# Three products of high and low parts for the softmax attentions, and an earlier start of the third block of w_out

## The chip, the cores and the metric

The kernel runs on one core of one Trainium2 chip. The metric is the device time of one execution in microseconds, as the median of several runs. The profile is one more execution of the same program, recorded by the hardware profiler.

## What is computed

Two layers of a hybrid decoder trunk over 256 positions of width 2048, all in float32. In each layer one projection of the normalised input feeds four groups of four heads: forgetting attention (fox), differential attention (diff), block-sparse attention (moba) and gated linear attention (GLA). Each group's output is multiplied by a SiLU gate, the four are joined and mapped back by w_out. Cut to what the change touches:

```python
def forgetting_attention(q, k, v, log_f):      # head width 128, 128-query blocks
    logits = einsum("bhqd,bhkd->bhqk", q_i, k) * scale + c_i[..., :, None] - cum[:, :, None, :]
    logits = where(k_pos <= q_pos, logits, -inf)
    return einsum("bhqk,bhkd->bhqd", softmax(logits), v)

p = softmax(q1 k1^T) - lam * softmax(q2 k2^T)  # differential attention, causal
diff = einsum("bhqk,bhkd->bhqd", p, v)

# block-sparse attention: with 256 positions there is one block of 256 keys,
# so each query attends to its own block, causally
moba = einsum("bhql,bhld->bhqd", softmax(where(own_pos <= q_pos, q k^T * scale, -inf)), v)

mixed = concatenate([fox, diff, moba, gla], axis=-1)
x = x + einsum("bse,ed->bsd", mixed, w_out)
```

## The kernel before

**Two kinds of product.** A large product (projection by w_in, output by w_out) is made of three F32R products of high and low parts: a weight tile `raw` that arrives by DMA is rounded into `hi` by ScalarE (`hi_of`, L399), the rest goes into `lo` by VectorE (`lo_of`, L402), and the input side stands ready as two tiles as well (`hTp` for the normalised input, `mTh` and `mTl` for the mixed output). `multiply` (L1194) issues hi by high, hi by low and lo by high. The small products of the attentions (scores and P V) take plain F32 operands, one `matmul` each (L275).

**The weight stream.** `_blocks` (L95) lists for each layer 17 column blocks of w_in and four of w_out (the last of the second layer is cut in two). A block sums 16 k tiles of 128 rows, in steps of two k tiles for a block of 512 columns, 12 products a step, and of four for narrower blocks. `_steps` (L131) orders the steps. Blocks with a `turn` go together: a turn's cut points say after which k tiles of a block the others have their turn. For w_out the turn is `(12,)` for the blocks 0 and 1, and the k tiles come in the order of the groups 3, 0, 1, 2 (GLA, fox, diff, moba). So the first 12 k tiles of block 0 go first, then the first 12 of block 1, then the last four of block 0 and of block 1, which are moba's, then the blocks 2 and 3. A block accumulates in one of two PSUM tiles `mm`, or, for one block of w_in whose `"side"` is set (L1082), in one of the two `side` tiles that the attentions use.

**Tasks between steps.** The rest of a layer runs as Python generators in `tasks`. After each step `tick` (L258) lets each task go on to its next `yield`, as long as the instructions that they have issued on VectorE and ScalarE cost no more, by a model, than the PE time issued so far. `prepare` (L1249) issues the split of the step three ahead, and at most four steps have parts. If a step needs k tiles that no task has finished yet, the loop at L1287 lets the tasks run on without PE steps between.

**Steps of a softmax group.** `projected` (L489) takes a projection out of PSUM, rotates it where needed, and turns it by 32x32 transposes and a transfer through DRAM (`turned`, `moved`, L284 and L297). For the queries `natural_of` (L481) makes one more copy into the plain order. `softmax` (L721) issues 12 score products a layer, `normalised` (L780) and `turned_p` (L763) divide and turn P, and `attend_columns` (L793) issues the 12 P V products of fox and moba, after it has waited for the values and the gate. `diff` (L890) issues its own, with 64-row score products that the change leaves alone, and 12 P V products. The values come out of PSUM in `fox_first`, `fox_v` and `rows_v` (L821, L832, L881), one ScalarE copy for each half of the rows. A group's output goes into its four k tiles of `mTh` and `mTl` in `split_group` (L524).

**Buffers.** `s4` has nine slots of 1024 elements a partition (`T4`), `s2` seven of 512 (`T2`). P turned is the fixed tile `pT`, which `env["pT"]` hands from one group to the next. GLA's masked queries are the fixed tile `tq` (L329), cleared once at the start on GpSimd (L1150); before that its space holds part of the first inputs.

Of the kernel before, what the change touches and what calls it, by code (L numbers as in the profile page):

```python
# [13 lines left out]
F32 = mybir.dt.float32  # L14
# [23 lines left out]
X_AT = (24, 28, 32, 36)  # L38
T4 = 9
T2 = 7  # L40
LAND = 5
# [53 lines left out]
def _blocks():  # L95

    def block(w, l, c0, n, kind, groups=(0, 1, 2, 3), turn=None):
        kts = [g * 4 + i for g in groups for i in range(4)]
        return {"w": w, "l": l, "c0": c0, "n": n, "kind": kind, "kts": kts, "per": 4 if n * 4 <= STEP_W else 2, "turn": turn}

    out = []
    for l in range(DEPTH):
        for i, (c0, n) in enumerate((
            (COL["gla_a"], 264),
            (COL["gla_g"] + 248, 264),
            (COL["gla_q"], 512),
            (COL["gla_v"], 512),
            (COL["fox_v"] + 258, 258),
            (COL["fox_q"], 512),
            (COL["fox_k"], 512),  # L110
            (COL["diff_q"], 512),
            (COL["diff_k"], 512),
            (COL["fox_v"], 258),
            (COL["fox_g"], 512),
            (COL["diff_v"], 512),
            (COL["moba_q"], 512),
            (COL["moba_k"], 512),
            (COL["diff_g"], 512),
            (COL["moba_g"], 512),
            (COL["moba_v"], 512),  # L120
        )):
            out.append(block("w_in", l, c0, n, "rows", turn=(l, (4, 8, 12)) if i < 3 else None))
        for chunk in range(4):
            cut = l + 1 == DEPTH and chunk == 3
            out.append(block("w_out", l, chunk * 512, 256 if cut else 512, "rows", (3, 0, 1, 2),
                             turn=(DEPTH + l, (12,)) if chunk < 2 else None))
    out.append(block("w_out", DEPTH - 1, D - 256, 256, "apart", (3, 0, 1, 2)))
    return out
# [35 lines left out]
class Costed:  # L164
# [5 lines left out]
    def __getattr__(self, name):  # L170
        f = getattr(self.eng, name)

        def call(*args, **kw):
            n = max(int(np.prod(a.shape[1:])) for a in args if hasattr(a, "shape"))
            self.us += self.fixed + self.per * n
            return f(*args, **kw)  # L176

        return call


# [25 lines left out]
def hybrid_trunk(  # L206
# [33 lines left out]
    s8 = Slots(wk, "eight", 1)  # L240
    sgs = Slots(wk, "gate", 2)
    side = Slots(sd, "side", 2)

# [31 lines left out]
    def matmul(out, lhsT, rhs, start, stop, tiles=1):  # L275
        left["pe"] += int(np.prod(rhs.shape[1:])) * (4 if lhsT.dtype == F32 else 1) / 2400.0 / tiles
        t_.matmul(out, lhsT, rhs, start=start, stop=stop)  # L277

    def transpose(out, src):
# [48 lines left out]
    ls2 = cp.tile([P, DEPTH, 2], F32, name="ls2")  # L328
    tq_flat = cp.tile([P, 2 * NL * P], F32, name="tq")  # L329
    tq = tq_flat.rearrange("p (m l x c) -> p m l x c", m=2, l=NL, x=2)  # L330
    one = cp.tile([P, 1], F32, name="one")
# [100 lines left out]
    def make_hT(l, chunk, parts):  # L432
# [23 lines left out]
        squares(l, chunk, parts)  # L456
        yield from moved(t, 2, X_LAND)
        tk = t.rearrange("p q j (k m) -> p k m (q j)", m=2)
# [29 lines left out]

    def projected(name, pool=None, heads_first=False, func=AF.Copy, turn=None, natural=None):  # L489

        def done(l, ps):
            nat = s4.get([P, 8, P])
            rows_of(l, ps, nat.rearrange("p (a m) d -> p m a d" if heads_first else "p (m a) d -> p m a d", m=2), func)
            tasks.append(run(l, nat))
            return nat

        def run(l, nat):
            yield
            if turn is not None:
                yield from rotated(nat, *turn)  # L500
            t = yield from turned([nat], pool or s4, lambda: s4.put(nat))
            if natural:
                t = yield from natural_of(t, s4, natural)
                yield
            env[name, l] = t
            ready.add((name, l))

        return done

    def rotated(nat, name, half, width):  # L510
# [99 lines left out]
    def gla(l, an):  # L610
        yield from until("constants")
        yield
        ps = yield from take_side()
# [31 lines left out]
        for pair in range(2):  # L645
# [56 lines left out]
            side.put(px)  # L702
        s4.put(env["gla_qk", l])
        s2.put(cum)
        yield from until(("gla_v", l))
# [15 lines left out]
    def softmax(qT, kT, scale, su, forget):  # L721
# [3 lines left out]
        for m in range(2):  # L725
            for kt in range(m + 1):
                dst = S[m][:, kt]
                for h in range(H):
                    matmul(dst[:, h], qT[:, m * H + h], kT[:, :, kt * H + h], True, True)
        s4.put(qT, kT)  # L730
        yield
# [48 lines left out]
    def normalised(p0, p1, su):  # L780
# [10 lines left out]
        return t  # L791

    def attend_columns(l, gi, name, qT, kT, forget=None):  # L793

# [4 lines left out]
        yield from until((name + "_v", l))  # L799
        yield from until((name + "_g", l))  # L800
        yield
        vn, sgT = env[name + "_v", l], env[name + "_g", l]
        ops = yield from take_side()
        o = ops.rearrange("p (h t) -> p h t", h=H)
        for h in range(H):
            v0, v1 = vn[:, 0, h * P:(h + 1) * P], vn[:, 1, h * P:(h + 1) * P]
            matmul(o[:, h, :P], v0, t[:, h], True, True)
            matmul(o[:, h, P:], v0, t[:, H + 2 * h], True, False)
            matmul(o[:, h, P:], v1, t[:, H + 2 * h + 1], False, True)
        s4.put(vn)  # L810
        env["pT"] = t
        yield
        mixed = yield from s4.take([P, H, SEQ])
        by_q = [z.rearrange("p h (m q j) -> p q (h m) j", m=2, q=4) for z in (mixed, o)]
# [4 lines left out]
        yield from split_group(l, gi, mixed, lambda: s4.put(mixed))  # L819

    def fox_first(l, ps):  # L821
        r = env["r", l]
        vn = s4.get([P, 2, GW])
        fx = sm.tile([P, 2, H], F32, name="fx", bufs=2)
        for m in range(2):
            v_.tensor_scalar(fx[:, m], ps[m][:, 254:258], r[:, m:m + 1], None, op0=OP.mult)
            a_.activation(vn[:, m, 258:], ps[m][:, :254], AF.Copy, scale=r[:, m:m + 1])
        env["fox_v", l] = vn
        tasks.append(fox(l))
        tasks.append(fox_forget(l, fx))  # L830

    def fox_v(l, ps):  # L832
        r, vn = env["r", l], env["fox_v", l]
        for m in range(2):
            a_.activation(vn[:, m, :258], ps[m], AF.Copy, scale=r[:, m:m + 1])
        ready.add(("fox_v", l))
# [44 lines left out]
    def rows_v(name):  # L881
        def done(l, ps):
            vn = s4.get([P, 2, GW])
            rows_of(l, ps, vn)
            env[name, l] = vn
            ready.add((name, l))

        return done

    def diff(l):  # L890
# [6 lines left out]

        def product(dst, i, h, m, kt):
            rows = slice(i * 64, i * 64 + 64)
# [12 lines left out]
        for h in range(H):  # L912
            for i in range(2):
                product(S[:, i, h], i, h, 0, 0)
        yield
# [17 lines left out]
        for kt in range(2):  # L933
            for h in range(H):
                for i in range(2):
                    product(T[i][:, kt, h], i, h, 1, kt)
        s4.put(qT, kT)
# [31 lines left out]
        yield  # L969
        vn = env["diff_v", l]  # L970
        ops = yield from take_side()
        o = ops.rearrange("p (m h d) -> p m h d", m=2, h=H)
        for h in range(H):
            matmul(o[:, 0, h], z[:, h], vn[:, 0, h * P:(h + 1) * P], True, True)
        for h in range(H):
            matmul(o[:, 1, h], z[:, H + 2 * h], vn[:, 0, h * P:(h + 1) * P], True, False)
            matmul(o[:, 1, h], z[:, H + 2 * h + 1], vn[:, 1, h * P:(h + 1) * P], False, True)
        s4.put(vn)
        env["pT"] = z
        yield  # L980
# [75 lines left out]
    for l in range(DEPTH):  # L1056
# [3 lines left out]
            gla_first, gla_gate, gla_qk, gla_v, fox_first,  # L1060
            projected("fox_q", natural=whole),
            projected("fox_k"),
            projected("diff_q", turn=turn_d, natural=whole),
# [3 lines left out]
            rows_v("diff_v"),  # L1067
            projected("moba_q", turn=turn_m, natural=whole),
            started(moba, projected("moba_k", turn=turn_m)),
            diff_gate,  # L1070
# [7 lines left out]
    for z in _BLOCKS:  # L1078
        l, f = next(dones)
        blocks.append({"kind": z["kind"], "lhs": hT if z["w"] == "w_in" else mT, "n": z["n"], "per": z["per"], "done": f and partial(f, l),  # L1080
                       "keys": {("r", l)}, "need": "h" if z["w"] == "w_in" else "m", "l": l,
                       "side": z["turn"] is not None and z["c0"] == COL["gla_g"] + 248})  # L1082
    plan = []
# [6 lines left out]
    def bundle(half):  # L1090
        return (pT, tq_flat)[half][:, :first.shape[2]]

# [45 lines left out]
    def first_rms():  # L1138
# [5 lines left out]
        for c in range(4):  # L1144
            yield from until(("h", 0, c))
            if c == 0:
                for half in range(2):
                    a_.activation(xts[0][:, half * 2:half * 2 + 2].rearrange("p k t -> p (k t)"),
                                  bundle(half)[:, KT:KT + 2 * SEQ], AF.Square)
                g_.memset(tq, 0.0)  # L1150
                g_.memset(pT, 0.0)
# [178 lines left out]
```

## Time and profile before

| | us |
|---|---|
| median of 3 runs | 910.52 (910.34 to 910.62) |
| the profiled execution | 910.29 |
| its span, first to last instruction | 908.5 |
| PE busy | 898.7 |
| VectorE (DVE) busy | 632.6 |
| ScalarE (ACT) busy | 497.9 |
| GpSimd (POOL) busy | 91.1 |

PE is the matmul engine, PEld its weight loads, which overlap with its products. A record of the trace is one instruction; matmuls are pipelined, so that a record is longer than its share of the engine's time. The chain of the page follows the work that ended last back to its start, and gives each engine its share of it.

### The profile page before, as it was taken

How to read it: one execution, taken by the hardware profiler on the slowest of the kernel's cores; microseconds unless marked ns; L12 is line 12 of the kernel's file. 1: busy time of each engine (PE TensorE's matmuls, PEld its weight loads, DVE VectorE, ACT ScalarE, POOL GpSimd, SP SyncE). 2: the span in 40 equal slices, each digit the busy share in tenths (PEclk: the TensorE clock that was granted, in tenths of full speed). 3: DMA queues.
4: the chain of work that ended last, by engine and by line, in shares of the span. 5: the costliest groups of instructions: out<-in, count | busy, mean ns of one | idle time of the engine just before them, and what ended most of it. 6: DMA issues, size and time to landing. Idle time of an engine off the chain costs nothing.

```text
span 908.5 us, 12645 instructions
## 1 busy us (share of the span) xinstructions
PE 898.7 (99%) x4678; PEld 766.0 (84%) x4678; DVE 632.6 (70%) x972; ACT 497.9 (55%) x679; POOL 91.1 (10%) x149
## 2 busy tenths in 40 slices
PE   9999999999999999999999999999999999999996
PEld 7989888898888888888899898888888888888886
DVE  7756778688568667746764658886875785695662
ACT  7576754465455357445665674644645545654441
POOL 1010011120101111001200101012200001220000
PEclk9999999999999999999999999999999999999999
DMA  9776576677747757758965756676866576686552
GB/s 325 246 235 195 183 267 223 214 234 210 250 141 232 231 187 228 231 170 260 295 198 178 239 172 238 184 229 214 254 218 199 162 234 200 216 270 213 187 165 93
DMA packets 56508, 195.78 MB, mean 215 GB/s; under 512 B 7637, under 2 KB 7933, under 8 KB 56446
## 3 DMA queue, kind: packets, MB, share of 16 engines
q1 hardware_dynamic: 45760, 164.47, 55.9%
q0 software_dynamic: 9616, 29.38, 11.3%
q10 hardware_dynamic: 1070, 1.14, 0.4%
q8 instruction: 36, 0.59, 0.3%
q14 instruction: 26, 0.21, 0.1%
HBM read 179.74 MB, written 15.21 MB: 215 GB/s over the span
## 4 chain that ended last, share of the span: by engine, by line
PE 98%; issue 1%; DMA 1%; DVE 0%; ACT 0%; POOLq 0%; POOL 0%; DVEq 0%; SPq 0%; ACTq 0%
PE mm L277 89%; PE side L277 9%; DMA tq<-in_first 1%; PE side L281 0%; DVE xs L176 0%; DVE hTp L176 0%; ACT hi L176 0%; DVE lo L176 0%; POOLq L1326 0%; POOL rf L397 0%; ACT two L176 0%; ACT hTp L176 0%; DVEq L1326 0%; SPq L1111 0%; DVE ssf L176 0%
## 5 line engine op out<-in xcount | busy, mean ns | idle before, releaser
L176 DVE TENSOR_TENSOR lo<-raw,hi 128x1024 fp32r<-128x1024 f32 (+2 forms) x299 | 364.8, 1224 | 236.2 <-ACT hi L176 234.1
L176 ACT ACTIVATE hi<-raw 128x1024 fp32r<-128x1024 f32 (+2 forms) x299 | 316.8, 1062 | 367.3 <-PE mm L277 318.4
L277 PE MATMUL mm<-hi,hTp 128*128 128x512 f32 (+2 forms) x2048 | 465.5, 371 | 0.1
L277 PEld LDWEIGHTS mm<-hi,hTp 128*128 128x128 f32 x2048 | 358.3, 188 | 65.9 <-issue 0.7
L277 PE MATMUL mm<-lo,hTp 128*128 128x512 f32 (+2 forms) x1024 | 249.8, 369 | 0.2
L277 PEld LDWEIGHTS mm<-lo,hTp 128*128 128x128 f32 x1024 | 181.0, 188 | 33.2 <-DVE lo L176 0.6
L277 PE MATMUL mm<-hi,mTh 128*128 128x512 f32 (+1 forms) x256 | 95.2, 376 | 0.0
L277 PE MATMUL mm<-hi,mTl 128*128 128x512 f32 (+1 forms) x256 | 95.0, 376 | 0.0
L277 PE MATMUL mm<-lo,mTh 128*128 128x512 f32 (+1 forms) x256 | 64.4, 376 | 0.0
L305 POOL DMA_DIRECT2D four<-turn x84 | 46.0, 554 | 102.3 <-DMA turn<-four 51.7
L277 PEld LDWEIGHTS mm<-hi,mTh 128*128 128x128 f32 x256 | 48.2, 188 | 8.7
L277 PEld LDWEIGHTS mm<-hi,mTl 128*128 128x128 f32 x256 | 48.2, 188 | 8.7
L277 PEld LDWEIGHTS mm<-lo,mTh 128*128 128x128 f32 x256 | 46.2, 188 | 8.7
L301 POOL DMA_DIRECT2D turn<-four x21 | 12.1, 577 | 320.0 <-DVE four L176 319.9
L176 DVE STREAM_TRANSPOSE pT<-four 32x128 f32<-32x128 f32 (+1 forms) x116 | 39.3, 350 | 1.0
L176 ACT ACTIVATE four<-mm,rstd 128x512 f32<-128x512 f32 (+2 forms) x56 | 33.5, 646 | 3.6 <-DVE fx L176 3.5
L176 ACT ACT_TABLE_LOAD x24 | 30.8, 1283 | 3.3 <-DVE an L176 3.0
L277 PEld LDWEIGHTS side<-four,four 128*128 128x128 f32 (+1 forms) x224 | 21.4, 190 | 1.9 <-issue 1.4
L277 PE MATMUL side<-four,four 128*128 128x128 f32 (+1 forms) x224 | 22.7, 277 | 0.0
L176 DVE STREAM_TRANSPOSE four<-four 128x1024 f32<-128x1024 f32 x18 | 22.3, 1240 | 0.3
L176 ACT ACTIVATE four<-side,nb 128x256 f32<-128x256 f32 (+1 forms) x48 | 20.6, 446 | 1.3 <-DVE nb L176 1.2
L176 DVE COPY_PREDICATED four<-masks,side 128x128 f32<-128x128 uint8 x56 | 19.1, 342 | 2.1 <-PE side L277 0.3
(149 smaller groups left out, 536.9 us busy)
## 6 DMA issues: line engine op xcount, KB each, us to landing
raw<-in_weights SPq DMA_DIRECT2D x272, 512.0 KB, 4.2
turn<-four POOLq DMA_DIRECT2D x21, 512.0 KB, 4.7
four<-turn POOLq DMA_DIRECT2D x84, 128.0 KB, 4.5
raw<-in_weights SPq DMA_DIRECT2D x16, 516.0 KB, 4.4
raw<-in_weights SPq DMA_DIRECT2D x15, 528.0 KB, 4.9
turn<-gate POOLq DMA_DIRECT2D x4, 512.0 KB, 5.5
gate<-turn POOLq DMA_DIRECT2D x16, 128.0 KB, 5.6
four<-in_xt SPq DMA_DIRECT2D x3, 512.0 KB, 6.5
```

The lines of the kernel that those rows point to most:

```text
L176: return f(*args, **kw)
L277: t_.matmul(out, lhsT, rhs, start=start, stop=stop)
L301: g_.dma_start(via, t.rearrange("p c a b -> p c (a b)"))
L305: g_.dma_start(t[c * 32:(c + 1) * 32].rearrange("p q a b -> p q (a b)"), via[:, c].rearrange("(q i) e -> i q e", q=4))
```

## The change

The scores of fox and moba and the P V of fox, diff and moba become sums of three F32R products:

```diff
+    def pairs(a, b):
+        return [(a[0], b[0]), (a[0], b[1]), (a[1], b[0])]
+
+    def product(out, a, b, start=True, stop=True):
+        both = pairs(a, b)
+        for i, (x, y) in enumerate(both):
+            matmul(out, x, y, start and i == 0, stop and i == len(both) - 1)
...
-                    matmul(dst[:, h], qT[:, m * H + h], kT[:, :, kt * H + h], True, True)
+                    product(dst[:, h], qT(m * H + h), kT(kt * H + h))
...
-            matmul(o[:, h, :P], v0, t[:, h], True, True)
-            matmul(o[:, h, P:], v0, t[:, H + 2 * h], True, False)
-            matmul(o[:, h, P:], v1, t[:, H + 2 * h + 1], False, True)
+            product(o[:, h, :P], v0, t(h))
+            product(o[:, h, P:], v0, t(H + 2 * h), stop=False)
+            product(o[:, h, P:], v1, t(H + 2 * h + 1), start=False)
...
-            matmul(o[:, 0, h], z[:, h], vn[:, 0, h * P:(h + 1) * P], True, True)
+            product(o[:, 0, h], z(h), vn((0, h)))
```

An `Operand` holds the two tiles and gives the two parts of one piece. The queries and keys of fox and moba are split after they are turned (for the queries this takes the place of `natural_of`), P after it is turned, the values as they leave PSUM:

```diff
+    def in_parts(t, side_of):
+        if side_of == "k":
+            hi = yield from s4.take(t.shape, F32R)
+            hi_of(hi, t)
+            yield
+            lo = yield from s4.take(t.shape, F32R)
+            lo_of(lo, t, hi)
+            s4.put(t)
+            return Operand((hi, lo), lambda n: (hi[:, :, n], lo[:, :, n]))
+        hi = yield from s4.take([P, t.shape[2], P], F32R)
+        lo = yield from s4.take([P, t.shape[2], P], F32R)
+        by_q = [z.rearrange("p n (q j) -> p q n j", q=4) for z in (hi, lo)]
+        for q in range(4):
+            hi_of(by_q[0][:, q], t[:, q])
+        yield
+        for q in range(4):
+            lo_of(by_q[1][:, q], t[:, q], by_q[0][:, q])
+        s4.put(t)
+        return Operand((hi, lo), lambda n: (hi[:, n], lo[:, n]))
...
+    def p_operand(t, vn):
+        h0 = yield from s2.take([P, H, P], F32R)
+        h1 = yield from s4.take([P, 2 * H, P], F32R)
+        hi_of(h0, t[:, :H])
+        hi_of(h1, t[:, H:])
+        yield
+        lo = yield from tqs.take([P, 3 * H, P], F32R)
+        lo_of(lo[:, :H], t[:, :H], h0)
+        lo_of(lo[:, H:], t[:, H:], h1)
+        env["pT"] = t
+        yield
+        return Operand((h0, h1, lo), lambda n: (h0[:, n] if n < H else h1[:, n - H], lo[:, n]))
...
+    def parts_of_v(l, ps, vn, c, to):
+        r = env["r", l]
+        for m in range(2):
+            a_.activation(vn[0][:, m, to], ps[m][:, c], AF.Copy, scale=r[:, m:m + 1])
+        for m in range(2):
+            v_.scalar_tensor_tensor(vn[1][:, m, to], ps[m][:, c], r[:, m:m + 1], vn[0][:, m, to].bitcast(F32), op0=OP.mult, op1=OP.subtract)
```

In `attend_columns` the wait for the gate stays ahead of P V for fox alone, and stands behind it for moba. `tq` becomes a slot of its own (`tqs`) that GLA takes and clears in each layer and gives back after its products, and that then holds the low part of P. The counts of the slots change, and a chunk's wait:

```diff
-T4 = 9
-T2 = 7
+T4 = 10
+T2 = 5
...
+    tqs = Slots(wk, "tq", 1)
...
-        yield from moved(t, 2, X_LAND)
+        yield from moved(t, 2, X_LAND if chunk else LAND)
...
+        tq_flat = yield from tqs.take([P, 2 * NL * P])
+        g_.memset(tq_flat, 0.0)
...
-                g_.memset(tq, 0.0)
+                tqs.put(first_tq)
```

Of w_out's third block the first four k tiles (GLA's) are put ahead of moba's k tiles of the blocks 0 and 1, and its sum is held in a `side` tile:

```diff
-                             turn=(DEPTH + l, (12,)) if chunk < 2 else None))
+                             turn=(DEPTH + l, ((12, 12), (12, 12), (0, 4, 4))[chunk]) if chunk < 3 else None))
...
-                       "side": z["turn"] is not None and z["c0"] == COL["gla_g"] + 248})
+                       "side": (z["w"], z["c0"]) in (("w_in", COL["gla_g"] + 248), ("w_out", 1024))})
```

More of the change, by code (lines that the diff above doesn't have):

```diff
@@ L178, in __getattr__, with __init__, __call__ @@
         return call
+class Operand:
+    def __init__(self, tiles, get):
+        self.tiles, self.get = tiles, get
+    def __call__(self, n):
+        return self.get(n)
 class Slots:
@@ L328, in hybrid_trunk @@
     ls2 = cp.tile([P, DEPTH, 2], F32, name="ls2")
-    tq_flat = cp.tile([P, 2 * NL * P], F32, name="tq")
-    tq = tq_flat.rearrange("p (m l x c) -> p m l x c", m=2, l=NL, x=2)
+    first_tq = tqs.get([P, 2 * NL * P])
     one = cp.tile([P, 1], F32, name="one")
@@ L487, in natural_of, with projected @@
         return z
-    def projected(name, pool=None, heads_first=False, func=AF.Copy, turn=None, natural=None):
+    def projected(name, pool=None, heads_first=False, func=AF.Copy, turn=None, natural=None, side_of=None):
         def done(l, ps):
@@ L504, in run @@
                 yield
+            elif side_of:
+                t = yield from in_parts(t, side_of)
+                yield
             env[name, l] = t
@@ L611, in gla @@
         yield from until("constants")
+        tq_flat = yield from tqs.take([P, 2 * NL * P])
+        g_.memset(tq_flat, 0.0)
+        tq = tq_flat.rearrange("p (m l x c) -> p m l x c", m=2, l=NL, x=2)
         yield
@@ L703, in gla @@
         s4.put(env["gla_qk", l])
+        tqs.put(tq_flat)
         s2.put(cum)
@@ L728, in softmax @@
                 for h in range(H):
-                    matmul(dst[:, h], qT[:, m * H + h], kT[:, :, kt * H + h], True, True)
-        s4.put(qT, kT)
+                    product(dst[:, h], qT(m * H + h), kT(kt * H + h))
+        s4.put(*qT.tiles, *kT.tiles)
         yield
@@ L791, in normalised, with release_p @@
         return t
+    def p_operand(t, vn):
[8 more added lines that the diff above has]
+        env["pT"] = t
+        yield
+        return Operand((h0, h1, lo), lambda n: (h0[:, n] if n < H else h1[:, n - H], lo[:, n]))
+    def release_p(p):
+        s2.put(p.tiles[0])
+        s4.put(p.tiles[1])
+        tqs.put(p.tiles[2])
     def attend_columns(l, gi, name, qT, kT, forget=None):
@@ L799, in attend_columns @@
         yield from until((name + "_v", l))
-        yield from until((name + "_g", l))
+        t = yield from p_operand(t, env[name + "_v", l])
+        if forget is not None:
+            yield from until((name + "_g", l))
         yield
-        vn, sgT = env[name + "_v", l], env[name + "_g", l]
+        vn = env[name + "_v", l]
         ops = yield from take_side()
@@ L805, in attend_columns @@
         for h in range(H):
-            v0, v1 = vn[:, 0, h * P:(h + 1) * P], vn[:, 1, h * P:(h + 1) * P]
-            matmul(o[:, h, :P], v0, t[:, h], True, True)
-            matmul(o[:, h, P:], v0, t[:, H + 2 * h], True, False)
-            matmul(o[:, h, P:], v1, t[:, H + 2 * h + 1], False, True)
-        s4.put(vn)
-        env["pT"] = t
+            v0, v1 = vn((0, h)), vn((1, h))
+            product(o[:, h, :P], v0, t(h))
+            product(o[:, h, P:], v0, t(H + 2 * h), stop=False)
+            product(o[:, h, P:], v1, t(H + 2 * h + 1), start=False)
+        s4.put(*vn.tiles)
+        release_p(t)
         yield
+        yield from until((name + "_g", l))
+        sgT = env[name + "_g", l]
         mixed = yield from s4.take([P, H, SEQ])
@@ L819, in attend_columns @@
         yield from split_group(l, gi, mixed, lambda: s4.put(mixed))
+    def parts_of_v(l, ps, vn, c, to):
[4 more added lines that the diff above has]
+            v_.scalar_tensor_tensor(vn[1][:, m, to], ps[m][:, c], r[:, m:m + 1], vn[0][:, m, to].bitcast(F32), op0=OP.mult, op1=OP.subtract)
     def fox_first(l, ps):
         r = env["r", l]
-        vn = s4.get([P, 2, GW])
+        vn = s4.get([P, 2, GW], F32R), s4.get([P, 2, GW], F32R)
         fx = sm.tile([P, 2, H], F32, name="fx", bufs=2)
@@ L826, in fox_first @@
             v_.tensor_scalar(fx[:, m], ps[m][:, 254:258], r[:, m:m + 1], None, op0=OP.mult)
-            a_.activation(vn[:, m, 258:], ps[m][:, :254], AF.Copy, scale=r[:, m:m + 1])
-        env["fox_v", l] = vn
+        parts_of_v(l, ps, vn, slice(0, 254), slice(258, 512))
+        env["fox_v", l] = Operand(vn, lambda z: tuple(y[:, z[0], z[1] * P:(z[1] + 1) * P] for y in vn))
         tasks.append(fox(l))
@@ L832, in fox_v @@
     def fox_v(l, ps):
-        r, vn = env["r", l], env["fox_v", l]
-        for m in range(2):
-            a_.activation(vn[:, m, :258], ps[m], AF.Copy, scale=r[:, m:m + 1])
+        parts_of_v(l, ps, env["fox_v", l].tiles, slice(0, 258), slice(0, 258))
         ready.add(("fox_v", l))
@@ L882, in done @@
         def done(l, ps):
-            vn = s4.get([P, 2, GW])
-            rows_of(l, ps, vn)
-            env[name, l] = vn
+            vn = s4.get([P, 2, GW], F32R), s4.get([P, 2, GW], F32R)
+            parts_of_v(l, ps, vn, slice(None), slice(None))
+            env[name, l] = Operand(vn, lambda z: tuple(y[:, z[0], z[1] * P:(z[1] + 1) * P] for y in vn))
             ready.add((name, l))
@@ L896, in diff, with score @@
         su = [sm.tile([P, 2, H], F32, name="su") for _ in range(2)]
-        def product(dst, i, h, m, kt):
+        def score(dst, i, h, m, kt):
             rows = slice(i * 64, i * 64 + 64)
@@ L913, in diff @@
             for i in range(2):
-                product(S[:, i, h], i, h, 0, 0)
+                score(S[:, i, h], i, h, 0, 0)
         yield
@@ L935, in diff @@
                 for i in range(2):
-                    product(T[i][:, kt, h], i, h, 1, kt)
+                    score(T[i][:, kt, h], i, h, 1, kt)
         s4.put(qT, kT)
@@ L970, in diff @@
         vn = env["diff_v", l]
+        z = yield from p_operand(z, vn)
+        yield
         ops = yield from take_side()
@@ L973, in diff @@
         for h in range(H):
-            matmul(o[:, 0, h], z[:, h], vn[:, 0, h * P:(h + 1) * P], True, True)
+            product(o[:, 0, h], z(h), vn((0, h)))
         for h in range(H):
[L976 to L979, printed above, removed]
+            product(o[:, 1, h], z(H + 2 * h), vn((0, h)), stop=False)
+            product(o[:, 1, h], z(H + 2 * h + 1), vn((1, h)), start=False)
+        s4.put(*vn.tiles)
+        release_p(z)
         yield
@@ L1060, in hybrid_trunk @@
             gla_first, gla_gate, gla_qk, gla_v, fox_first,
-            projected("fox_q", natural=whole),
-            projected("fox_k"),
+            projected("fox_q", side_of="q"),
+            projected("fox_k", side_of="k"),
             projected("diff_q", turn=turn_d, natural=whole),
@@ L1067, in hybrid_trunk @@
             rows_v("diff_v"),
-            projected("moba_q", turn=turn_m, natural=whole),
-            started(moba, projected("moba_k", turn=turn_m)),
+            projected("moba_q", turn=turn_m, side_of="q"),
+            started(moba, projected("moba_k", turn=turn_m, side_of="k")),
             diff_gate,
@@ L1090, in bundle @@
     def bundle(half):
-        return (pT, tq_flat)[half][:, :first.shape[2]]
+        return (pT, first_tq)[half][:, :first.shape[2]]
     def x_of(kt):
```

## The prediction

> **What bounds the kernel now.** I read the page from its top: busy times, then the forty slices, then the chain that ended last.
>
> ```profile
> span 908.5 us, 12645 instructions
> ...
> PE 898.7 (99%) x4678; PEld 766.0 (84%) x4678; DVE 632.6 (70%) x972; ACT 497.9 (55%) x679; POOL 91.1 (10%) x149
> ...
> PEclk9999999999999999999999999999999999999999
> ...
> PE 98%; issue 1%; DMA 1%; DVE 0%; ACT 0%; POOLq 0%; POOL 0%; DVEq 0%; SPq 0%; ACTq 0%
> ```
>
> The matmul engine holds 98% of the chain, at full clock from end to end. Nothing else is ever the last to arrive for long, so a microsecond put into or taken out of PE's stream moves the end by a microsecond, and work on DVE or ACT costs nothing until it makes PE wait. The question is therefore how long PE takes for the products that the change rewrites. They stand in the groups of PE by form, and their pace in the chain in order of time.
>
> ```profile
> L277 PE MATMUL side<-four,four 128*128 128x128 f32 x128 | 16.2, 275 | 0.0
> ...
> L277 PE MATMUL side<-pT,four 128*128 128x128 f32 x96 | 11.4, 275 | 0.0
> ...
> L277 PE MATMUL side<-four,pT 128*128 128x128 f32 x48 | 5.7, 275 | 0.0
> ```
> ```profile
> 43.74 2.91 PE side L277 x24
> 46.65 10.89 PE mm L277 x48
> ...
> 150.83 3.12 PE side L277 x28
> ...
> 251.82 2.68 PE side L277 x24
> ...
> 381.83 2.68 PE side L277 x24
> ```
>
> By the code a layer has 12 score products in fox, 12 in moba, and 12 P V products in each of fox, moba and diff: 60, in two layers 120. The rows pT,four (fox and moba P V, 48 products) and four,pT (diff, 24) show 96 and 48 records, so each plain F32 product is two records. The row four,four holds the 48 score products as 96 records and GLA's 16 products on sT as 32, and the latter stay. The change touches 240 records. In the chain 24 of them take 2.68 us: **111.7 ns a record, 223 ns a product**, 240 x 0.1117 = **26.8 us** now. (275 ns is the pipelined length of one record; the chain gives the pace.)
>
> **The change, part by part.** *The products.* Each F32 product of 128 columns becomes three F32R products of 128 columns: 360 instead of 120. No F32R product in this trace has fewer than 256 columns, so the pace at 128 has to be bounded.
>
> From below, by streaming: in the chain 24 products of 264 columns take 2.91 us, 121.3 ns each, and 48 of 512 take 10.89, 226.9 ns each. The line through both has a slope of 0.426 ns a column and gives 63.4 ns at 128 columns. If columns were all that counted, 360 x 0.0634 = 22.8 us, 4.0 us less than now.
>
> But each product also loads its 128x128 stationary operand. The loads (PEld) around a sum in which two F32 products have one column each show what a load takes when there is nothing to stream; the rows are the timeline asked in narrow windows, each starting one load later.
>
> ```profile
> 37.43 0.50 PE L277 MATMUL side<-one,four 128*128 128x1 f32 x4
> ...
> 37.43 0.41 PEld L277 LDWEIGHTS side<-one,four 128*128 128x128 f32 x3
> ...
> 37.54 0.30 PEld L277 LDWEIGHTS side<-one,four 128*128 128x128 f32 x2
> ...
> 37.65 0.19 PEld L277 LDWEIGHTS side<-one,four 128*128 128x128 f32 x1
> 37.76 0.30 PEld L277 LDWEIGHTS mm<-hi,hTp 128*128 128x128 f32 x2
> ...
> 37.87 0.43 PEld L277 LDWEIGHTS mm<-hi,hTp 128*128 128x128 f32 x2
> ```
>
> Loads start at 37.43, 37.54, 37.65, 37.76 and 37.87: one every 0.11 us, though a record streams one column. The last two are F32R loads (hi, hTp), and the second starts 0.11 us after the first, as soon as the F32 ones did. So a load takes the port 0.11 us in F32R too, longer than the 63 ns of streaming: at 128 columns **the weight load sets the pace**, at the 111.7 ns that the F32 records of 128 columns also keep. `product` uses its first operand's high part twice in a row; that a load is saved there is excluded by the last block of w_out ("apart"), which does the same:
>
> ```profile
> L277 PE MATMUL mm<-four,mTh 128*128 128x256 f32 x32 | 5.8, 283 | 0.0
> ...
> L277 PEld LDWEIGHTS mm<-four,mTh 128*128 128x128 f32 x32 | 5.0, 192 | 0.0
> ```
>
> 32 products, 32 loads. So I take 111.7 ns: 360 x 0.1117 = 40.2 us, **13.4 us more** than 26.8. Around it: 0.105 us (the rounding of 0.11) gives 37.8, +11.0 us; the 121.3 ns of the narrowest stretch above, if a fixed part of an F32R product comes on top of the load, gives 43.7, +16.9 us. The upper bound is that a short F32R product runs as an F32 one does, in two records: 360 x 0.2234 = 80.4 us, +53.6 us. I take the loads because they are measured on the very operation.
>
> The page "TensorE: Matmul & The Clock Gate" of the Trainium skill, section "Weight-path perf modes — Fast Weight Load (FWL) and DoubleRow", says that a faster weight load is on for 128 weights whenever the type is not FP32. If F32R counted as another type, the stream would set the pace and the change would gain the 4.0 us. The F32R loads 0.11 us apart speak against it. Its section "Back-to-back issue gap" gives some 81 ns for a product of 128 columns in a stream of loads and products; an estimate by it is 360 x 0.081 - 26.8 = +2.4 us, and no F32R row here is that fast.
>
> *The splits.* High parts go to ACT, low parts to DVE.
>
> ```profile
> L176 DVE TENSOR_TENSOR lo<-raw,hi 128x1024 fp32r<-128x1024 f32 x268 | 326.4, 1222 | 209.2 <-ACT hi L176 207.5 <-issue 0.3
> ...
> L176 DVE SCALAR_TENSOR_TENSOR hTp<-four,ngt,hTp 128x256 fp32r<-128x256 f32 x24 | 12.7, 590 | 0.0
> ...
> L176 DVE TENSOR_TENSOR two<-two,rs 128x512 f32<-128x512 f32 x4 | 2.8, 691 | 0.1
> ```
> ```profile
> L176 ACT ACTIVATE hi<-raw 128x1024 fp32r<-128x1024 f32 x268 | 283.6, 1061 | 330.2 <-PE mm L277 287.9 <-DMA raw<-in_weights 13.8 <-DVE lo L176 7.1
> ...
> L176 ACT ACTIVATE four<-mm,rstd 128x512 f32<-128x512 f32 x48 | 30.0, 676 | 0.0
> ...
> L176 ACT ACTIVATE hTp<-four,ngt 128x256 fp32r<-128x256 f32 x24 | 13.6, 640 | 0.2 <-DMA four<-in_xt 0.2
> ```
>
> Per softmax group on DVE: k 1.22, q four quarters of 0.59, P 0.69 + 1.22, V two of 0.69: 6.9 us; diff has P and V, 3.3. Two layers: 4 x 6.9 + 2 x 3.3 = 34 us. ACT by its rows: k 1.06, q 4 x 0.64 less the one copy of about 1.06 that it replaces, P 0.68 + 1.06: 4.3 us, diff 1.7, together 21 us. DVE rises from 633 to 667 us, 72% of the new span, ACT to 56%. DVE's idle time before lo<-raw is spent on ACT, whose own idle time is spent on PE: both run as far ahead as the four part buffers let them, three steps of 12 x 0.227 = 2.72 us, and that cover, 8 us, swallows bursts of 2 us. Cost 0; without the cover up to the 34 us of DVE would show.
>
> *The buffers.* tq becomes a slot that GLA takes, clears and gives back, and the low part of P uses it. GLA's last products with tq are the 28 records at 150.83 in the chain, fox's P V stands at 251.82, so in a layer the two users are 100 us apart. Two clears are added on POOL, of the kind that the tile view of pT shows at 1.39 us:
>
> ```profile
> L1151 POOL MEMSET pT<- x1: 1387/1387/1387, 12.8 to 12.8; 128x1536 f32 x1
> ```
>
> POOL is 10% busy; behind the clear wait only its own DMA issues, and GLA's first use of tq lies several steps on. Cost 0, at worst their 2 x 1.4 us. T4 from 9 to 10 and T2 from 7 to 5 move waits of tasks, not of PE; I price them with the second rival.
>
> *The third block.* PE's work is the same, in another order: the first four k tiles of w_out's third block (two steps, 5.4 us) come ahead of the last four of the first two. It buys time for moba, the last group to be ready. Now:
>
> ```profile
> 362.63 0.39 PE L277 MATMUL mm<-hi,mTh 128*128 128x512 f32 x1
> ```
> ```profile
> 370.92 0.40 DVE L176 STREAM_TRANSPOSE pT<-four 32x256 f32<-32x256 f32 x1
> ...
> 391.38 1.22 DVE L176 TENSOR_TENSOR mTl<-four,mTh 128x1024 fp32r<-128x1024 f32 x1
> ```
>
> w_out begins at 362.6; 12 steps and the P V of 2.68 later, at 398.0, PE needs moba's k tiles, which are whole at 392.6: 5.4 us early. The change puts that need off by 5.4 us and by the longer P V (1.3), to a margin of 12.1 us, and delays the tiles: two more yields for k (each at least a step, 5.4 us), and two to three for P's split (5.4 to 8.2), partly in the 10 us between the last transpose (371.3) and P V, in which the task now waits for its gate as well. Delay 5.4 to 13.6 us against 12.1: I take it as covered, cost 0, at most 1.5 us a layer if every step goes against it. Nothing is gained either, since PE waits for none of this now.
>
> Sum: the profiled execution took 910.3 us (908.5 of span and 1.8 around it); + 13.4 = 923.7, and with the 0.2 that the median of the three runs (910.5) lies above it, **923.9 us**.
>
> **Rivals.** *Streaming sets the pace* (the other side): if the loads of these products hide behind something that the five starts above do not show, the 360 products go at 63 to 74 ns and the kernel ends at 906.5 or up to 910.5. It decides at 26.8 / 360 = 74 ns. For it speaks only that loads and products overlap everywhere; against it the 0.11 us between loads. *Moba comes late*: each step by which it misses costs 2.72 us of PE; with the 1.5 of above 4.2 a layer, 8.4 in all, 932.3. For it: margin and delay are alike in size, ten slots of "four" must hold two tiles where there was one, and DVE has more to do. *Two records a product*: 964.1 us; nothing in the trace excludes it, but the wider F32R products all are one record, and their loads are no longer. *The split saves nothing and costs nothing* would need a pace of exactly 74 ns, and no row has it.
>
> **How the numbers follow.** The loads' pace, with moba in time (921.5 to 927.4): 0.68. Moba late, to 936: 0.12. Two records: 0.11. Streaming: 0.06. Something between, about 913: 0.03. The range 920 to 936 leaves out the last three, 0.20; its lower end is 921.5 less the run-to-run share of 0.2%, about what a measurement of this kernel can tell from no change. Faster by more than that: 0.05 (streaming, but for its slow end); within it: 0.02; slower: 0.93.
>
> **What would show it.** Right: each changed stretch has 36 records where it had 24 and takes 4.0 us instead of 2.68, PE still holds 98% of the chain, DVE near 667 us, and moba's k tiles begin without an idle PE. Wrong: stretches of 2.3 us (streaming), of 8 us or with 72 records (two records), or PE idle ahead of moba's k tiles, with DVE mTl as its releaser.

## The result and the profile after

The changed kernel takes **924.06 us** (median of 4 runs, 923.96 to 924.16) against 910.56 for the kernel before on the same chip: a ratio of 1.0149, 95% interval 1.0137 to 1.0161, or 13.5 us more. Its profiled span is 922.4 us. The page's first part and the heads of the chain:

```profile
span 922.4 us, 12981 instructions
...
PE 912.7 (99%) x4798; PEld 780.0 (85%) x4798; DVE 659.1 (71%) x1020; ACT 507.8 (55%) x703; POOL 95.3 (10%) x150
...
PEclk9999999999999999999999999999999999999999
...
PE 98%; issue 1%; DMA 1%; DVE 0%; ACT 0%; POOLq 0%; POOL 0%; DVEq 0%; SPq 0%; ACTq 0%
```

PE bounds the kernel as before, at the same clock, and simply has more to do: 120 records more (240 became 360) and 14.0 us more busy. DVE rose by 26.5 us and ACT by 9.9, and neither appears in the chain. The chain in order of time (start, duration, what) shows where the time went:

```profile
184.71 3.97 PE side L288 x36
...
262.73 2.83 PE mm L288 x12
...
392.89 3.97 PE side L288 x36
396.86 8.27 PE mm L288 x36
405.13 5.44 PE side L288 x24
410.57 10.88 PE mm L288 x48
```

There are ten such stretches, five a layer. Each has 36 records and 3.97 us where it had 24 and 2.68, 1.29 us more. The first step behind one is some 0.1 us longer too: twelve 512-column products take 2.83 us at 262.73, where the pace of the 48 at 410.57 (0.2267 us each) gives 2.72. The first load of a stretch hides under the wide product ahead of it, and the first wide product behind it waits for its own: around the stretch at 392.89, PE's timeline starts the first two short products 0.06 us apart (392.73 and 392.79) and the first two wide ones behind them 0.29 us apart (396.70 and 396.99). That is 0.06 of the 0.1 us; the rest is spread over the step and stays open. 10 x (1.29 + 0.1) = 13.9 us, the whole growth of the span (922.4 - 908.5). The medians lie 13.5 us apart, because the profiled execution of the kernel before, at 910.29, is 0.3 us under its median. The line at 405.13 is the third block's early start, 24 products into `side`, ahead of moba's k tiles at 410.57.

### The profile page after: what moved, and what is told of

It reads as the page before. It is cut to its first block, busy times and chain, and to the rows that moved or that the text cites. A ratio compares the mean times of both kernels' runs of the same rounds, so it can differ in the third digit from the quotient of the medians.

```text
span 922.4 us, 12981 instructions
## 1 busy us (share of the span) xinstructions
PE 912.7 (99%) x4798; PEld 780.0 (85%) x4798; DVE 659.1 (71%) x1020; ACT 507.8 (55%) x703; POOL 95.3 (10%) x150
## 4 chain that ended last, share of the span: by engine, by line
PE 98%; issue 1%; DMA 1%; DVE 0%; ACT 0%; POOLq 0%; POOL 0%; DVEq 0%; SPq 0%; ACTq 0%
PE mm L288 83%; PE side L288 15%; DMA tq<-in_first 1%; PE side L300 0%; DVE xs L176 0%; DVE lo L176 0%; ACT hi L176 0%; POOLq L1403 0%; POOL rf L415 0%; ACT two L176 0%; DVE hTp L176 0%; ACT hTp L176 0%; DVEq L1403 0%; SPq L1188 0%; DVE ssf L176 0%
## 5 line engine op out<-in xcount | busy, mean ns | idle before, releaser
L288 PE MATMUL mm<-hi,mTh 128*128 128x512 f32 (+1 forms) x192 | 70.2, 372 | 0.0
L288 PE MATMUL mm<-hi,mTl 128*128 128x512 f32 (+1 forms) x192 | 70.1, 372 | 0.0
L288 PE MATMUL mm<-lo,mTh 128*128 128x512 f32 (+1 forms) x192 | 47.3, 371 | 0.0
L288 PE MATMUL side<-four,four 128*128 128x128 f32 (+1 forms) x368 | 46.6, 276 | 0.0
L288 PEld LDWEIGHTS side<-four,four 128*128 128x128 f32 (+1 forms) x368 | 42.6, 191 | 1.9 <-issue 1.4
L288 PEld LDWEIGHTS mm<-hi,mTl 128*128 128x128 f32 x192 | 36.2, 188 | 6.3
L288 PEld LDWEIGHTS mm<-hi,mTh 128*128 128x128 f32 x192 | 36.2, 188 | 6.2
L176 ACT ACTIVATE four<-mm,rstd 128x512 f32<-128x512 f32 (+3 forms) x56 | 33.3, 645 | 3.3 <-DVE fx L176 3.2
L288 PE MATMUL side<-hi,mTh 128*128 128x512 f32 x64 | 24.9, 389 | 0.0
L288 PE MATMUL side<-hi,mTl 128*128 128x512 f32 x64 | 24.9, 389 | 0.0
```

## The experiments

**The theory:** at 128 columns an F32R product costs its weight load, 0.11 us, so three of them cost 0.335 us against 0.223 for one F32 product, and all else that the change adds is covered. **The rivals:** F32R streams its columns twice when there are fewer than 256 (which gives nearly the same price at 128 columns); the splits and buffers have a share; the third block costs or saves something of its own.

**The disputed cost by itself.** Ten kinds of 24 products each, into a PSUM tile that nobody reads, in the middle of the first layer, each between stretches of 512 columns; operands from `hTp`, and each kind on a line of its own:

```diff
+            t_.matmul(ps[:, :128], h5[:, j % 8, :128], h5[:, 8 + j % 8, :128], start=True, stop=True)
...
+            t_.matmul(ps[:64, :128], h5[:, j % 8, :64], h5[:, 8 + j % 8, :128], start=True, stop=True)
```

> Ten kinds of 24 F32R products each, into a PSUM tile that nobody reads, between stretches of 24 products of 512 columns; read from the chain, not from the total. If the weight load sets the pace: 128-column weights with 64, 128, 192 or 224 streamed columns all take 2.65 to 2.75 us for 24 (0.111 each), 256 columns 2.9; weights of 64 or 32 columns with 128 streamed columns fall to the stream's 1.5 to 1.7; the same weights 24 times over still 2.7. Rival, F32R of fewer than 256 columns streams each column twice (two times 0.426 ns): 128 columns 2.6, but 192 columns 3.9 and 224 columns 4.6, and 64-column weights with 128 columns still 2.6.

Its chain, from the one execution that there is, at a mean granted clock of 0.998; the columns streamed are 512 (L1138), 128 (L1140), 64 (L1144), 192 (L1148), 224 (L1152) and 256 (L1156) under 128-column weights, then 128 columns under weights of 64 (L1160) and of 32 columns (L1164), 256 under 64 (L1168), and 128 with the same 128-column weights 24 times over (L1172):

```profile
194.46 5.46 PE side L1138 x24
199.92 2.63 PE side L1140 x24
...
208.10 2.60 PE side L1144 x24
...
216.25 2.66 PE side L1148 x24
...
224.38 2.67 PE side L1152 x24
...
232.53 2.87 PE side L1156 x24
...
240.87 1.44 PE side L1160 x24
...
247.84 1.45 PE side L1164 x24
...
254.81 2.73 PE side L1168 x24
...
263.00 2.63 PE side L1172 x24
```

From 64 to 224 columns the time stays at 2.60 to 2.67 us, 0.108 to 0.111 a product: the columns don't matter, the load does. Streaming twice would have made 192 columns 3.9 us, so that rival falls. With weights of half the width the same 128 columns take 1.44 us, 0.060 each, and weights of 32 columns save nothing more: there the stream sets the pace, near the 63 ns that the prediction's line through the wide products gave. At 256 columns load and stream are nearly alike: 2.87 us with full weights (0.120 a product), 2.73 with half of them. Repeating the weights saves nothing.

**The load's price in the kernel.** Three runs that change the number of products or of loads. One gives diff its F32 products back, without its splits:

```diff
-            product(o[:, 0, h], z(h), vn((0, h)))
+            matmul(o[:, 0, h], z[:, h], vn[:, 0, h * P:(h + 1) * P], True, True)
```

> The changed kernel with diff's P V in plain F32 again: 24 products instead of 72, and P and the values of diff not split. Theory (only the products on PE count): 24 x 0.1117 = 2.7 us less, 921.4. Rival (the splits on DVE and ACT have a share): more than 3.5 us less, under 920.5.

One keeps only the product of the high parts:

```diff
-        return [(a[0], b[0]), (a[0], b[1]), (a[1], b[0])]
+        return [(a[0], b[0])]
```

> The changed kernel with only the product of the high parts; the two cross products are left out, the splits stay. Theory (0.1117 us for each F32R product of 128 columns): 240 products fewer, 26.8 us less, 897.3. Rival (a fixed cost per sum, or the splits): nearer to 905.

And one makes the scores of the second half of the rows wide: both key tiles of a head stream under one load of its queries, the same columns with half the loads:

```diff
+        for h in range(H):
+            k2 = [z[:, :, h::H].rearrange("p q n j -> p n q j") for z in kT.tiles]
+            product(two[:, h], qT(H + h), k2)
```

> The changed kernel with the scores of the second half of the rows as products of 256 columns (both key tiles under one load of the queries): the same streamed columns, 48 loads of 128x128 fewer in 16 heads. Theory (the load sets the pace): per head 6 x 0.1117 become 3 x 0.1203, 0.31 us less, 16 heads 4.9 us, 919.1. Rival (streamed columns set it): 924.1.

| run | us | ratio to the kernel before, 95% interval |
|---|---|---|
| diff plain | 921.30 | 1.0119 (1.0104 to 1.0134) |
| high parts only | 897.33 | 0.9856 (0.9841 to 0.9870) |
| wide scores | 919.12 | 1.0096 (1.0079 to 1.0113) |

Expected were 921.4, 897.3 and 919.1. The third is the one that separates loads from columns. In its chain a score stretch has 12 products of 128 columns and 12 of 256 where it had 36 of 128:

```profile
184.66 2.80 PE side L288 x24
```

2.80 us instead of 3.97, with not one column fewer.

**The splits, slots and clears.** All of them as in the changed kernel, but one F32 product of the high parts; the low parts are made and not used:

```diff
-        both = pairs(a, b)
+        both = [(a[0].bitcast(F32), b[0].bitcast(F32))]
```

> The changed kernel with all its splits, buffers and order, but one F32 product of the high parts in place of the three; the low parts are made and not used. Theory (splits, slots and clears are covered): the time before, 910.6 within 0.3%. Rival (they cost PE time): above 913.

910.47 us, ratio 1.0000 (0.9990 to 1.0009). Its page:

```profile
PE 898.6 (99%) x4678; PEld 766.0 (84%) x4678; DVE 658.9 (73%) x1020; ACT 507.3 (56%) x703; POOL 94.7 (10%) x150
```

DVE carries the changed kernel's load (658.9 and 659.1 us), PE that of the kernel before, and the time is the one of before. So the 26 us of DVE and 9 of ACT cost nothing, and the products cost everything.

**The third block.** Alone on the kernel before, and taken out of the changed kernel:

```diff
-                             turn=(DEPTH + l, (12,)) if chunk < 2 else None))
+                             turn=(DEPTH + l, ((12, 12), (12, 12), (0, 4, 4))[chunk]) if chunk < 3 else None))
```

> The kernel before with only the third block begun earlier. Theory: PE waited for nothing there, so 910.5 within 0.2%. Rival (the side tile that it holds delays the tasks, or the order of the weights costs): above 912.5.

> The changed kernel with the old order of w_out. In its trace moba's k tiles are whole at 405.05 and would be needed at 405.13 without the third block's 5.4 us. Theory (the block is cover for a delay that the splits made): a miss of up to one step a layer, 924.5 to 929.5, with PE idle before mm<-hi,mTh. Rival (the block covers nothing): 924.1 within 0.2%. Rival (it covers all of its 5.4 us a layer): 935.

Alone it gives 910.59 us, ratio 1.0002 (0.9993 to 1.0012). Without it the changed kernel takes 924.23, ratio 1.0151 (1.0134 to 1.0168), which can't be told from 924.06. So the theory of the second run (924.5 to 929.5) missed, and its first rival holds: the splits don't make moba late even without the block. The order of the work neither costs nor saves anything here. But without the block nothing is to spare. VectorE's row of moba's low part and PE's first products with moba's k tiles, in the run without the block:

```profile
403.78 1.22 DVE L176 TENSOR_TENSOR mTl<-four,mTh 128x1024 fp32r<-128x1024 f32 x1
```
```profile
404.92 0.39 PE L288 MATMUL mm<-hi,mTh 128*128 128x512 f32 x1
405.15 0.40 PE L288 MATMUL mm<-hi,mTl 128*128 128x512 f32 x1
```

The low part is whole at 405.00 and first used at 405.15. In the changed kernel it is whole at 405.05, by this row, and needed at 410.57:

```profile
403.83 1.22 DVE L176 TENSOR_TENSOR mTl<-four,mTh 128x1024 fp32r<-128x1024 f32 x1
```

To see what that margin is worth, both got one more step of delay ahead of moba's split:

```diff
-        yield
+        for _ in range(2 if forget is None else 1):
+            yield
         yield from split_group(l, gi, mixed, lambda: s4.put(mixed))
```

> The changed kernel with one more step (2.72 us) of delay ahead of the split of moba's output. Theory (the third block leaves a margin of 5.5 us: whole at 405.05, needed at 410.57): still in time, 924.1 within 0.2%. Rival (the margin is used up): 926.5 to 929.5.

> The same delay without the third block, where the margin is 0.1 us: PE should miss moba's k tiles by up to 2.6 us a layer, 925.5 to 929.5, with an idle PE before mm<-hi,mTh or mTl. Less than 1 us in all would mean that the loop which lets the tasks run on when a step is not ready takes the delay back.

With the third block 923.99 us (1.0149, 1.0133 to 1.0166), as expected. Without it **932.50** (1.0240, 1.0224 to 1.0255), outside what was expected and 8.3 us above 924.2. PE's timeline in that run:

```profile
404.83 0.39 PE L288 MATMUL mm<-hi,mTh 128*128 128x512 f32 x1
407.68 0.66 PE L288 MATMUL mm<-hi,mTl 128*128 128x512 f32 x1 [2.46 <-DVE mTl L176]
408.14 0.63 PE L288 MATMUL mm<-hi,mTh 128*128 128x512 f32 x1
408.57 0.63 PE L288 MATMUL mm<-hi,mTl 128*128 128x512 f32 x1
...
411.89 0.39 PE L288 MATMUL mm<-hi,mTh 128*128 128x512 f32 x1
```

One product goes ahead (the high part was there), then PE waits 2.46 us for DVE, and then its products start 0.43 us apart instead of 0.227. The step that begins at 404.83 would have ended 2.72 us later, at 407.55; the next one begins at 411.89. That is 4.3 us late in this layer: the second product starts 2.6 us later than it would have, and the other 1.7 are the slow products behind it.

**Better than the sum of three.** Wide scores and wide P V (both row tiles of P under one load of the first values) on the changed kernel, then the same with diff plain:

> The same done to P V of fox and moba too (both row tiles under one load of the first values): another 4.9 us less, 914.2; rival 924.1. Three pieces of P's high part instead of two, three of the low, cost nothing if DVE and ACT stay covered.

> Wide scores and wide P V for fox and moba, and diff's P V in plain F32 again: the two savings should add up, 914.0 - 2.7 = 911.2, still above 910.5, because each head keeps three products of 128 columns (3 x 0.1117) where one F32 product takes 0.2234. Rival (the parts of the sum interact, by waits): 912.5 or more.

They took 913.97 us (1.0038, 1.0023 to 1.0053) and 911.10 (1.0008, 0.9999 to 1.0017). The savings add up as expected, and end a little above the kernel before or level with it, since each head keeps its three products of 128 columns. So the last run mixes the two kinds: three F32R products where 256 columns share a load, one F32 product where there are 128 columns.

```diff
-            product(o[:, h, :P], v0, t(h))
-            product(o[:, h, P:], v0, t(H + 2 * h), stop=False)
-            product(o[:, h, P:], v1, t(H + 2 * h + 1), start=False)
+            product(o[:, h], v0, t(h), stop=False)
+            matmul(o[:, h, P:], vn[2][:, h * P:(h + 1) * P], t.tiles[2][:, H + 2 * h + 1], False, True)
```

Here `t(h)` gives the 256 columns of both row tiles, `vn[2]` and `t.tiles[2]` are unsplit F32, and the scores are done in the same way.

> Three F32R products only where 256 columns share a load (second half of the rows in the scores, the first values in P V), one plain F32 product where there are 128 columns; diff plain. Per head and side 0.2234 + 3 x 0.1197 = 0.583 instead of 3 x 0.2234 = 0.670 before: 0.087 less, 32 of them in two layers, 2.8 us under the kernel before, 907.7. Rival (F32 and F32R products in one PSUM sum, or the tighter slots, make PE wait): 910.5 or more.

**907.78 us**, ratio 0.9971 (0.9960 to 0.9983): 0.3% faster than the kernel before. Its first score and P V stretches in the chain hold 20 records, 8 of four F32 products and 12 wide ones:

```profile
184.58 2.35 PE side L288 x20
...
261.86 2.32 PE side L288 x20
```

Against 2.68 before and 3.97 after the change. The second score stretch of the layer, at 329.46, takes 2.53.

## Why the prediction was right

*What bounds the kernel.* Right. PE's share of the chain is 98% in both profiles, and the splits alone moved the time by nothing. This is what made a sum over one engine enough.

*The price of a short F32R product.* Right, and it carried the forecast: 0.1117 us from the F32 records and the spacing of the loads. The probe gives 0.110 at 128 columns and shows that it is the load. The step from five loads 0.11 us apart to "the load sets the pace" was the one that could have failed, since no F32R product under 256 columns was in the trace; streaming (906.5) and two records (964.1) were the two ways out, and the runs close both. The bound with a fixed part on top of the load (121.3 ns) is not reached: 192 and 224 columns take the bare load.

*The sum.* 40.2 - 26.8 = 13.4 us forecast, 13.5 measured by the medians and 13.9 by the spans. In detail a stretch takes 3.97 us instead of the forecast 4.02, and the step behind it some 0.1 us more, which the sum did not have: it counted 36 loads, and the one that it puts at the head of the stretch is paid behind it. Over ten stretches that is 0.5 us less and 1.0 us more; that the two nearly cancel is luck.

*The splits.* The cover was judged rightly, the sizes too high: DVE rose by 26.5 us where 34 were forecast, ACT by 9.9 where 21 were. The quarters of q were priced by the 590 ns of a strided row from another place, and these take less:

```profile
L176 DVE TENSOR_TENSOR four<-four,four 128x256 fp32r<-128x256 f32 x16 | 5.8, 425 | 0.0
```

By the means that is 16 x 0.165 = 2.6 us of the 7.5 on DVE; the rest is not broken down. On ACT the quarters were overpriced in the same way (408 ns, not 640). That is 16 x 0.23 = 3.7 us of the 11; another 5.1 are four table loads of 1.28 us that fell away, 20 where there were 24 (why is not shown):

```profile
L176 ACT ACT_TABLE_LOAD x20 | 25.7, 1283 | 3.3 <-DVE an L176 3.0
```

*The third block.* "Covered, cost 0" was right, and the forecast margin was not. It took 12.1 us and a delay of 5.4 to 13.6; the trace leaves 5.5 us, so the delay was 6.6, near its lower end. Where it arises can be read from PE's first product of w_out and DVE's last transpose of moba's P in the changed kernel:

```profile
368.25 0.39 PE L288 MATMUL mm<-hi,mTh 128*128 128x512 f32 x1
```
```profile
381.97 0.40 DVE L176 STREAM_TRANSPOSE pT<-four 32x256 f32<-32x256 f32 x1
```

The transpose ends 14.1 us behind w_out's first product, where it was 8.7 us in the kernel before (371.32 and 362.63): 5.4 us, the size of the two yields that the forecast gave to k. From there to P V it is 10.5 us in both kernels (to 381.83 before, to 392.89 after), so the two to three yields of P's split added nothing. The other 1.3 us are the longer P V itself, which the forecast counted in the margin and not in the delay. That P V no longer waits for moba's gate may be why the split found room; no run puts that wait back. The rival "moba comes late" did not come true, not even without the block, but it was near: a delay of one step more is swallowed with the block and costs 8.3 us without it. Its price was too low: 2.72 us for a missed step, where 4.3 a layer were measured.

## What to carry to other kernels

Here three F32R products of parts beat F32 only where the stream is as long as the weight load: 3 x 0.120 us with 256 columns behind each load of 128 columns, against 0.447 for the two F32 products of 128 columns that they replace, but 0.335 against 0.223 with 128. One F32 product of 256 columns in place of the two was not tried. The kernel before has such products only with 17 rows, two of them in four records, and its chain gives them 0.53 us each, more than the 0.447:

```profile
L277 PE MATMUL side<-at,wa 17*128 17x256 f32 x8 | 2.3, 400 | 0.0
```
```profile
63.21 1.06 PE side L277 x4
```

Look for products that share an operand and let it be the stationary one for all their columns before splitting them. And when an order of work buys time, measure the margin and not only the total: here the same total hid a margin of 5.5 us in one kernel and of 0.15 in the other.

## What the runs showed that was not expected

A wait of 2.46 us in PE's stream cost 4.3 us, because the clock fell behind it. The windows of the run without the third block and with the delay (duration, then PE, PEld, DVE, ACT and POOL busy, granted clock, DMA share, GB/s):

```profile
400.00:404.00 4.00, 4.00 (x20) 3.30 (x19) 2.22 (x2) 2.01 (x2) 0.00 (x0) 1.00 0.36 129
404.00:408.00 4.00, 1.54 (x7) 1.00 (x6) 2.36 (x2) 1.06 (x1) 0.00 (x0) 0.98 0.54 149
408.00:412.00 4.00, 4.00 (x12) 3.09 (x12) 0.00 (x0) 1.01 (x1) 0.00 (x0) 0.59 0.33 120
412.00:420.00 8.00, 8.00 (x37) 6.64 (x36) 3.68 (x3) 3.80 (x6) 1.27 (x1) 1.00 0.53 147
```

The granted clock is 0.59 from 408 to 412, right behind the wait, and full again from 412 on. Asked by single microseconds it is 0.93 from 407 to 408, 0.50 in each of the next three and 0.86 from 411 to 412, so PE had half its clock for some 3.4 us, and lost 1.7. The second layer's wait, 2.46 us as well, did the same (0.67 from 866 to 870). It may not happen every time: one of the four executions took 931.26 us, at a mean clock of 0.996, where the others took 932.38 to 932.68 at 0.994. By estimate from the 1.7 us, the clock fell behind one of its two waits only; that is not shown. The Trainium skill, page "TensorE: Matmul & The Clock Gate", section "Why this matters for your kernels", asks for no idle gaps over some 3 us; here one of 2.46 us was enough to lose the clock, so the measurement draws the line lower.
